# A hybrid decoder step on one core: where the accumulating transfers, the next block's tokens and a few copies are placed

## The chip, the cores and the metric

The kernel runs on one core of a Trainium2 chip. The metric is the time of one execution on the device in microseconds (us). Three runs of the kernel before took 2428.46, 2424.86 and 2425.33 us; the median is 2425.33.

## The reference

One inference step of a single decoder layer for 2048 prompt tokens and 64 sample tokens, width 1024, all in float32. An input projection feeds two mixers, a gated linear recurrence with matrix states (HGRN2) and a short gated convolution; an output projection, a layer norm, a feed-forward block and a second layer norm follow:

```python
mix = jnp.einsum('btm,md->btd', jnp.concatenate([o.astype(x.dtype), yc], axis=-1), w_out)
x = _layer_norm(ALPHA * x + mix, ln1_g, ln1_b)
hid = jnp.square(jax.nn.relu(jnp.einsum('btd,df->btf', x, w_ff1)))      # FF1, 1024 -> 4096
x = _layer_norm(ALPHA * x + jnp.einsum('btf,fd->btd', hid, w_ff2), ln2_g, ln2_b)   # FF2
```

## The kernel before

**Blocks and stages.** The prompt is worked off in four blocks of 512 tokens; block 1 also carries the 64 sample tokens. A block has two phases, each with a memory pool of its own. The "m" phase holds the input projections (`m1`, `m2`, `m3`), the recurrence that runs between their steps (`rec_step`), the output projection and the first layer norm. The "f" phase holds the feed-forward block. The hidden width is cut into eight chunks c of 512; chunks 0 and 1 are computed plainly at the start of the f phase (`pl["f0"]`), and then two parts follow, each with the rest of its four chunks: FF1 for them and then FF2 for all four. In time: block 0 has FF1 from about 290 us, FF2 from 333.9 to 428.1, FF1 to 515.2, FF2 to 597.0; the FF2 stages of block 1 are 993.3 to 1097.7 and 1188.5 to 1289.8, those of block 2 1613.7 to 1691.7 and 1772.3 to 1852.8.

**Precision by splitting.** Each float32 operand is split into a high part, copied by ScalarE (ACT) into the matmul's float32r type, and a low part, the rest, by VectorE (DVE): `wh`, `wl` for weights (lines 201 and 208), `h`, `l` for FF2's left operands, `X` for tokens, `hp` for sample operands (lines 162 and 163, in `split`). A product is three matmuls (high x high, high x low, low x high: lines 237 to 239, and 243 to 245 where several chains share a bank); the sample's pairs take two (248, 249). DVE's low parts are put into a list `later` and issued at the next `flush`, that is at the beginning of the next unit.

**Products by a fast scheme.** FF2 in every block, and FF1 in blocks 1 to 3, use a 2 x 2 scheme with seven products instead of eight, in this order:

```python
PRODUCTS = (("T4", "D"), ("B11", "A"), ("B21", "C"), ("T2", "A"), ("T1", "B"), ("T3", "A"), ("B22", "B"))
```

FF2 makes seven passes, one for each product, each over four chunks: 28 units of one weight tile each. After a pass's last chunk its two banks are added into the result tokens `x1` (`add_to`, lines 1229 and 1232), in T3 into two places each; four of the passes (`SAMPLE`) also have sample matmuls in block 1, and at their end `sample_sums` copies the upper half of a bank with ACT (`upper`, line 254, into a `TMP` tile) and adds both halves (lines 1240 to 1244). `sum_rows` forms FF2's left-hand sums (line 1221). `prepare` splits the left operand of a unit two units ahead into `h` and `l`, each in three buffers; in the f phase `TMP` takes its buffers from h's three.

**Sums of weights, made by transfers.** T1 to T4 are sums of weight quarters. They are made once, in HBM, by transfers from GpSimd's queue (POOL), some of which accumulate: `make_sums` yields after each. It makes T1 and T3 as copies, accumulates onto both, copies T3 to T2, accumulates, copies T2 to T4, accumulates. Every accumulation needs the transfer to the same tile before it: eight chunks, or six, earlier. `making` makes the 64 for FF2 (tiles T_b) during block 0's m phase; `making1` makes 48 for FF1 (six chunks, tiles T_a), which blocks 1 to 3 read. Before, `making1` is advanced three steps after each of the 8 units of block 0's first FF1 and two after each of the 16 of the second. Nothing in POOL's queue waits for those units, only for transfers.

**The weights' queue.** Weight and token tiles are "units" in one fixed list. SyncE's queue (SP) loads them into three `st` buffers, `unit_split` makes the parts, and `weights(i)` sees to it that units up to i + 3 are split. The next block's tokens are units too (`x_units`, four of them, a fifth for the sample ahead of block 1); `X_PLACES` says behind which FF2 units of the second part they stand. They take the `X` buffers that held this block's normed tokens. `norm_weights(1)` loads the second norm's `lnb` on SP's queue before the first FF2; that load has to wait for the last `affine` (line 943) of the first norm, and later weight loads stand behind it.

Of the kernel before, what the change touches and what calls it, by code (L numbers as in the profile page):

```python
# [9 lines left out]
F32 = mybir.dt.float32  # L10
# [3 lines left out]
ALU = mybir.AluOpType  # L14
AX = mybir.AxisListType

P = 128
# [28 lines left out]

SAMPLE = {"B21": (1, ((0, 1),)), "B11": (0, ((0, 1), (1, -1))), "T1": (0, ((1, 1),)), "B22": (1, ((1, 1),))}

X_PLACES = (("T3", 4), ("T3", 6), ("B22", 4), ("B22", 5), ("B22", 6))

QUARTER = {"B11": (0, 0), "B21": (1, 0), "B12": (0, 1), "B22": (1, 1)}

# [8 lines left out]
def hybrid_step(ctx, tc, a, o):  # L61
    nc = tc.nc
    v, s, g, te = nc.vector, nc.scalar, nc.gpsimd, nc.tensor

    cst = ctx.enter_context(tc.tile_pool(name="cst", bufs=1))
# [6 lines left out]
    def new(shape, tag, bufs, dt=F32, of=None):  # L72
        count[0] += 1
        return (of or pool).tile(list(shape), dt, tag=tag, bufs=bufs, name=f"{tag}{count[0]}")


    phase = {}
# [8 lines left out]
    def S(shape=(P, SLOT), dt=F32):  # L86
        assert phase["in"] == "m"
        return new(shape, "S", NSLOT, dt, phase["of"])

    def TMP():  # L90

        return S((P, 4, P)) if phase["in"] == "m" else new((P, 4, P), "h", 3, F32, phase["of"])

    def TOK(dt=F32):
        return new((P, D), "tok", 8, dt)
# [5 lines left out]
    def SM(shape):  # L101
        return new(shape, "sm", 16)
# [13 lines left out]
    small = cst.tile([P, 36], F32, name="small")  # L116
    lnb = cst.tile([P, 2, D], F32, name="lnb")
    nhalf = cst.tile([P, NH], F32, name="nhalf")
    halo = cst.tile([P, 4, 2], F32, name="halo")
    lw = cst.tile([P, 6, NH], F32, name="lw")  # L120
    lbl, onorm, convw = small[:, 0:4], small[:, 4:8], small[:, 8:20]
# [47 lines left out]
    def add_unit(src, scale=None, cols=D, use=None, spare=False):  # L169
        units.append((src, scale, cols, use, spare))  # L170
        return len(units) - 1
# [52 lines left out]
    def weights(i, kept=0):  # L224

        ahead(i + 4 - kept)
        return handles.pop(i)
# [4 lines left out]
    def pump():  # L232
        if bg:
            bg.pop(0)()
# [23 lines left out]
    def norm_weights(which):  # L258

        for i in range(2):  # L260
            nc.sync.dma_start(lnb[:, i, :], a["lnb"][:, 2 * which + i, :])
# [75 lines left out]
    def quarter2(c, k):  # L337
        return a["w_ff2"][c * 4 + RAW[k]] if k in RAW else sums[c][k]

    def make_sums(at, cs):  # L340
        for to, of, acc in (("T1", "B11", False), ("T3", "B22", False), ("T1", "B12", True), ("T3", "B12", True),
                            ("T2", "T3", False), ("T2", "B11", True), ("T4", "T2", False), ("T4", "B21", True)):
            for c in cs:
                if acc:
                    g.dma_start(at(c, to), at(c, of), accum_op=ALU.add, max_dma_last_dim=4096)
                else:
                    g.dma_start(at(c, to), at(c, of), max_dma_last_dim=4096)
                yield

    making = make_sums(quarter2, range(NCH))  # L350
    making1 = make_sums(quarter1, range(NPLAIN, NCH))

    for b in range(NB):
# [16 lines left out]
        for part in range(NCH // NPART):  # L370
# [9 lines left out]
            for step, _ in PRODUCTS:  # L380
                for c in cs:
                    ff2.append((step, c, add_unit(quarter2(c, step))))
                    if (step, c) in X_PLACES and nx:
                        src, cols, use = nx.pop(0)
# [13 lines left out]
    for b in range(NB):  # L398
# [20 lines left out]
        qs, ks, fs, scs, kds = {}, {}, {}, {}, {}  # L419
# [421 lines left out]
        def rec_step():  # L841
            nonlocal rec_done
            if not rec_done:
                rec_done = next(rec, 0) == 0

        def main():
            yield from m1()
            yield from m2()
            yield from m3()

        for i, _ in enumerate(main()):
            rec_step()
            if b == 0 and i >= 6:
                if i == 6:

                    g.tensor_tensor(SM((P, 1)), ks[0][:, 0:1], fs[0][:, 0:1], ALU.add)
                next(making, 0)
                next(making, 0)
            if i >= 16 and i % (3 if samp else 4) == 0:
                rec_step()  # L860
            if i % 2 == 0:
                pump()
# [71 lines left out]
        def drain():  # L934
            while lnq:
                before()
                after()
                flush()
# [71 lines left out]
        def F(shape, tag, bufs, dt=F32):  # L1010
            return new(shape, tag, bufs, dt, phase["of"])
# [10 lines left out]
        def values(c):  # L1022
            if c not in raw:

                raw[c] = F((P, 4, 2, 256), "raw", NPART)
            return raw[c]
# [170 lines left out]
        def prepare():  # L1197
            if not queue:
                return
            step, c = queue.pop(0)  # L1200
            r = raw[c]
            x = r[:, SLOT_OF[step]]
            h, l = F((P, 2, 256), "h", 3, F32R), F((P, 2, 256), "l", 3, F32R)
            split(h, l, x)
            hid[step, c] = (h, l)
            if step in SUMMED:
                assert (step, c) in summed
            seen.add((step, c))
            if step == PRODUCTS[-1][0]:
                del raw[c]  # L1210
# [35 lines left out]
        for part, (ff1_units, ff2_units) in enumerate(pl["parts"]):  # L1246
            queue += [(step, c) for step, c, _ in ff2_units]
            for i, (step, c, u) in enumerate(ff1_units):
                if i >= len(ff1_units) - 2:
                    prepare()  # L1250
                if b == 0:
                    if i == 0:
                        for _ in making:
                            pass
                    ff1(step, weights(u), segs)
                    for _ in range(3 - part):
                        next(making1, 0)
                else:
                    ff1_product(step, c, weights(u))
            drain()  # L1260
            if part == 0:
                norm_weights(1)
            else:
                xq.clear()
            sumq += [(k, c) for k in SUMMED for c in sorted({c for _, c, _ in ff2_units})]
            nsum = 0
            spairs = []
            squeue = [c * FC + 2 * SAMPLE[step][0] for step, c, _ in ff2_units if samp and step in SAMPLE]

            def sample_rows():  # L1270
                if squeue:
                    f = squeue.pop(0)
                    hp = F((P, 2, P), "hp", 2, F32R)
                    split(hp[:, :, 0:NS], hp[:, :, NS:P], sample_values(f // FC, f))
                    spairs.append(hp)

            banks = {}
            sample_rows()
            cfirst, clast = ff2_units[0][1], ff2_units[-1][1]
            for n_, (step, c, u) in enumerate(ff2_units):  # L1280
                w = weights(u)
                while sumq and (nsum * 3 + 6) // 2 <= n_:
                    sum_rows()
                    nsum += 1
                parts = [tuple(x[:, q * 512:q * 512 + 512] for x in w) for q in range(2)]
                prepare()
                if step in SAMPLE:
                    sample_rows()
                if pl["last"] and step == PRODUCTS[-1][0] and c >= NCH - 3:
                    if c == NCH - 3:  # L1290
                        last = [F((P, 4, 2, 256), "raw", NPART, F32R) for _ in range(2)]
                    for x in ((0, 2), (1, 3))[c - NCH + 3]:
                        split(last[0][:, x], last[1][:, x], raw[NCH - 1][:, x])
                k = to[step]
                first = k not in banks
                if first:
                    banks[k] = [PS() for _ in range(2)]
                h, l = hid.pop((step, c))
                for p in range(2):
                    cs = slice(p * P, p * P + P)  # L1300
                    for q, (rh, rl) in enumerate(parts):
                        mm3_on(banks[k][p], h[:, q, cs], l[:, q, cs], rh, rl, first and q == 0, c == clast and q == 1)
                if samp and step in SAMPLE:
                    if c == cfirst:
                        ys = PS()
                    hp = spairs.pop(0)
                    for q, (rh, rl) in enumerate(parts):
                        mm_pair(ys, hp[:, q, :], rh, rl, c == cfirst and q == 0, c == clast and q == 1)
                if c == clast:
                    for t0, dh, sign in INTO[k][step]:  # L1310
                        for p in range(2):
                            add_to(t0 + p, dh, banks[k][p], sign)
                    if samp and step in SAMPLE:
                        sample_sums(ys, SAMPLE[step][1])
# [4 lines left out]
        if b == NB - 1:  # L1319

            c = NCH - 1
            ws = [weights(u) for u in pl["last"]]
            flush_all()
            h, l = last
# [128 lines left out]
```

## Time and profile before

| What | us |
|---|---|
| median of three runs | 2425.33 |
| the profiled execution | 2427.2 |
| its span, first to last instruction | 2425.4 |
| TensorE (PE) busy | 2369.6 |
| VectorE (DVE) busy | 1729.7 |
| ScalarE (ACT) busy | 1212.1 |
| GpSimd (POOL) busy | 170.4 |

The times in the profile's rows come from the one profiled execution and count from its first instruction. A row of the timeline has start, duration, engine, line, operation, what it writes and reads, and in brackets how long the engine sat idle before it and what ended that. A row of waits has engine and line, whom it waited for, the sum in us, the number and the longest. A row of stretches has, after the stretch's bounds and length, the busy time of each engine, the granted share of TensorE's clock, the mean busy share of the core's 16 DMA engines, and GB/s. Rows of DMA queues give packets, MB and the share of the 16 engines' time (q1 is SP's queue with the weights, q0 POOL's); rows of issues give count, size and median us to landing.

### The profile page before, as it was taken

How to read it: one execution, taken by the hardware profiler on the slowest of the kernel's cores; microseconds unless marked ns; L12 is line 12 of the kernel's file. 1: busy time of each engine (PE TensorE's matmuls, PEld its weight loads, DVE VectorE, ACT ScalarE, POOL GpSimd, SP SyncE). 2: the span in 40 equal slices, each digit the busy share in tenths (PEclk: the TensorE clock that was granted, in tenths of full speed). 3: DMA queues.
4: the chain of work that ended last, by engine and by line, in shares of the span. 5: the costliest groups of instructions: out<-in, count | busy, mean ns of one | idle time of the engine just before them, and what ended most of it. 6: DMA issues, size and time to landing. Idle time of an engine off the chain costs nothing. (4 is left out here: it accounts for less than half of the span.)

```text
span 2425.4 us, 34901 instructions
## 1 busy us (share of the span) xinstructions
PE 2369.6 (98%) x13596; PEld 2062.5 (85%) x13596; DVE 1729.7 (71%) x2651; ACT 1212.1 (50%) x1898; POOL 170.4 (7%) x208
## 2 busy tenths in 40 slices
PE   8999989999999999899999999999999999999998
PEld 7888977887989889779977888998987888998996
DVE  7756648258775677775687856888588965888678
ACT  5234535355423446556654324665665324575563
POOL 2220321000001110000000000000000001000001
PEclk9999999999999999999999999999999999999999
DMA  8996999346223644444544325465566225456563
GB/s 294 273 273 213 286 280 284 115 136 200 100 65 84 164 153 131 158 154 160 172 147 140 100 70 182 152 205 186 179 191 191 99 76 170 141 196 193 182 189 116
DMA packets 128229, 412.40 MB, mean 170 GB/s; under 512 B 13184, under 2 KB 17664, under 8 KB 128064
## 3 DMA queue, kind: packets, MB, share of 16 engines
q1 hardware_dynamic: 105904, 342.19, 43.3%
q0 software_dynamic: 22016, 67.71, 11.1%
q8 instruction: 107, 1.75, 0.3%
q14 instruction: 58, 0.48, 0.1%
q10 hardware_dynamic: 144, 0.26, 0.0%
HBM read 399.07 MB, written 69.77 MB: 193 GB/s over the span
## 5 line engine op out<-in xcount | busy, mean ns | idle before, releaser
L208 DVE TENSOR_TENSOR wl<-st,wh 128x1024 fp32r<-128x1024 f32 x568 | 692.5, 1220 | 218.7 <-ACT wh L201 217.5
L201 ACT ACTIVATE wh<-st 128x1024 fp32r<-128x1024 f32 x569 | 600.4, 1055 | 401.5 <-PE ps L245 118.7
L237 PE MATMUL ps<-X,wh 128*128 128x256 f32 (+2 forms) x1504 | 515.2, 343 | 8.5 <-ACT X L162 8.0
L239 PE MATMUL ps<-X,wl 128*128 128x256 f32 (+2 forms) x1504 | 505.7, 336 | 0.3 <-DVE wl L208 0.3
L238 PE MATMUL ps<-X,wh 128*128 128x256 f32 (+2 forms) x1504 | 505.7, 336 | 0.3 <-DVE X L163 0.3
L245 PE MATMUL ps<-wh,l 128*128 128x512 f32 x868 | 345.3, 398 | 10.7 <-DVE l L163 10.4
L243 PE MATMUL ps<-wh,h 128*128 128x512 f32 x868 | 341.3, 393 | 10.3 <-ACT h L162 10.3
L244 PE MATMUL ps<-wl,h 128*128 128x512 f32 x868 | 341.2, 393 | 5.5 <-DVE wl L208 5.4
L237 PEld LDWEIGHTS ps<-X,wh 128*128 128x128 f32 x1504 | 286.2, 190 | 37.7 <-ACT X L162 8.9
L239 PEld LDWEIGHTS ps<-X,wl 128*128 128x128 f32 x1504 | 285.8, 190 | 27.5 <-DVE wl L208 0.7
L238 PEld LDWEIGHTS ps<-X,wh 128*128 128x128 f32 x1504 | 286.2, 190 | 26.2 <-DVE X L163 1.4
L245 PEld LDWEIGHTS ps<-wh,l 128*128 128x128 f32 x868 | 164.3, 189 | 60.5 <-DVE l L163 26.9
L243 PEld LDWEIGHTS ps<-wh,h 128*128 128x128 f32 x868 | 164.7, 190 | 44.3 <-ACT h L162 11.8
L244 PEld LDWEIGHTS ps<-wl,h 128*128 128x128 f32 x868 | 164.3, 189 | 42.3 <-DVE wl L208 7.8
L163 DVE TENSOR_TENSOR l<-raw,h 128x512 fp32r<-128x512 f32 x217 | 148.2, 683 | 19.7 <-ACT h L162 19.7
L269 POOL TENSOR_TENSOR sm<-sm,nhalf 128x1 f32<-128x1 f32 (+1 forms) x34 | 35.1, 1033 | 1579.5 <-DVE sm L268 1533.3
L162 ACT ACTIVATE h<-raw 128x512 fp32r<-128x512 f32 x217 | 133.6, 616 | 4.4 <-DVE tok L1244 2.3
L245 PE MATMUL ps<-X,wl 128*128 128x256 f32 (+1 forms) x432 | 124.9, 289 | 0.0
L243 PE MATMUL ps<-X,wh 128*128 128x256 f32 (+1 forms) x432 | 124.9, 289 | 0.0
L244 PE MATMUL ps<-X,wh 128*128 128x256 f32 (+1 forms) x432 | 124.9, 289 | 0.0
L1134 DVE TENSOR_TENSOR raw<-raw,ps 128x256 f32<-128x256 f32 (+1 forms) x96 | 50.4, 551 | 85.1 <-PE ps L245 84.9
L237 PE MATMUL ps<-wh,X 128*128 128x512 f32 x256 | 104.1, 407 | 0.0
(256 smaller groups left out, 4122.1 us busy)
## 6 DMA issues: line engine op xcount, KB each, us to landing
st<-in_w_ff SPq DMA_DIRECT2D x231, 512.0 KB, 3.6
st<-T_b SPq DMA_DIRECT2D x124, 512.0 KB, 3.9
st<-in_w_in SPq DMA_DIRECT2D x110, 512.0 KB, 3.5
st<-T_a SPq DMA_DIRECT2D x72, 512.0 KB, 3.6
st<-in_w_out SPq DMA_DIRECT2D x56, 512.0 KB, 4.5
T_b<-in_w_ff POOLq DMA_DIRECT2D x48, 512.0 KB, 18.4
T_a<-in_w_ff POOLq DMA_DIRECT2D x36, 512.0 KB, 23.7
T_b<-T_b POOLq DMA_DIRECT2D x16, 512.0 KB, 19.1
```

Of the source, the lines that this page charges most:

```text
L162: s.activation(hi, src, AF.Copy)
L163: later.append(lambda: v.tensor_tensor(lo, src, hi.bitcast(F32), ALU.subtract))
L201: s.activation(wh, st, AF.Copy)
L208: v.tensor_tensor(wl, st, wh.bitcast(F32), ALU.subtract)
L237: te.matmul(out, lh, rh, start=first, stop=False)
L238: te.matmul(out, lh, rl, start=False, stop=False)
L239: te.matmul(out, ll, rh, start=False, stop=last)
L243: te.matmul(out, lh, rh, start=first, stop=False, skip_group_check=True)
L244: te.matmul(out, lh, rl, start=False, stop=False, skip_group_check=True)
L245: te.matmul(out, ll, rh, start=False, stop=last, skip_group_check=True)
L269: g.tensor_tensor(st[:n, 15:16], st[:n, 14:15], nhalf[:n, 0:1], ALU.pow)
L1134: v.tensor_tensor(z, z, ps, (ALU.add, ALU.subtract)[op - 2])
```

## The change

Five edits. `hold` is a POOL addition of one column, x + x into a tile `tick`, that reads x and so waits for whoever writes x; POOL's later instructions stand behind it. In block 0's FF1, after each unit, one `hold` on the chunk's result and one step of `making1` (before: three or two steps without a read). In block 0's FF2, at each pass's first unit, a `hold` on that unit's h and one step. In block 1's projections one step at every second step of the loop. In all these are 24, 14 and up to 24 calls; the 48 transfers are used up in block 1. `TMP` in the f phase gets two buffers of its own. `X_PLACES` moves the tokens to one unit in a pass: behind chunk 6 of T4, B11, B21 and T3, and the fifth behind chunk 5 of B22 (before: two in T3 and the rest in B22). The first two `prepare` calls for FF2 come three FF1 units earlier. The `hold` helper also takes the place of one existing addition in block 0.

```diff
-X_PLACES = (("T3", 4), ("T3", 6), ("B22", 4), ("B22", 5), ("B22", 6))
+X_PLACES = (("T4", 6), ("B11", 6), ("B21", 6), ("T3", 6), ("B22", 5))
...
-        return S((P, 4, P)) if phase["in"] == "m" else new((P, 4, P), "h", 3, F32, phase["of"])
+        return S((P, 4, P)) if phase["in"] == "m" else new((P, 4, P), "tmp", 2, F32, phase["of"])
...
+    tick = cst.tile([P, 1], F32, name="tick")
...
+    def hold(x):
+
+        g.tensor_tensor(tick, x, x, ALU.add)
...
-                    g.tensor_tensor(SM((P, 1)), ks[0][:, 0:1], fs[0][:, 0:1], ALU.add)
+                    hold(ks[0][:, 0:1])
                 next(making, 0)
                 next(making, 0)
+            if b == 1 and i % 2 == 0:
+                next(making1, 0)
...
-                if i >= len(ff1_units) - 2:
+                if len(ff1_units) - 5 <= i < len(ff1_units) - 3:
                     prepare()
...
                     ff1(step, weights(u), segs)
-                    for _ in range(3 - part):
-                        next(making1, 0)
+                    hold(values(c)[:, 0, 0, 0:1])
+                    next(making1, 0)
...
                 h, l = hid.pop((step, c))
+                if b == 0 and n_ % 4 == 0:
+                    hold(h[:, 0, 0:1].bitcast(F32))
+                    next(making1, 0)
```

## The prediction

> **What bounds the kernel now.** I read the page first, then a table of stretches cut at the kernel's stages, then the waits and the timeline inside the stretches that were too long.
>
> ```profile
> span 2425.4 us, 34901 instructions
> PE 2369.6 (98%) x13596; PEld 2062.5 (85%) x13596; DVE 1729.7 (71%) x2651; ACT 1212.1 (50%) x1898; POOL 170.4 (7%) x208
> ```
>
> TensorE (PE) sets the end: it is busy 2369.6 of 2425.4 us, and the change leaves its matmuls as they are. So it can gain only what PE idles, about 56 us, plus slow matmuls after an idle. In the next rows the columns are stretch, PE, PEld, DVE, ACT, POOL busy, granted clock, DMA share, GB/s. The first row is most of block 0's way through FF1's start, the fourth its second FF1; all others are the second feed-forward product (FF2), 28 units of weights each: block 0 twice, block 1 twice, block 2 twice.
>
> ```profile
> 251.00:333.90 82.90, 82.90 (x524) 75.44 (x523) 45.69 (x56) 42.49 (x69) 24.75 (x32) 1.00 1.03 294
> 333.90:428.10 94.20, 82.32 (x337) 63.45 (x336) 64.93 (x81) 44.33 (x56) 14.87 (x18) 0.96 0.96 284
> 428.10:515.20 87.10, 87.10 (x386) 72.15 (x385) 25.13 (x24) 34.79 (x48) 0.00 (x0) 1.00 0.32 102
> 515.20:597.00 81.80, 79.66 (x338) 63.63 (x337) 68.13 (x86) 48.77 (x62) 0.00 (x0) 0.98 0.62 195
> 993.30:1097.70 104.40, 95.10 (x402) 76.86 (x402) 77.36 (x113) 50.84 (x79) 0.00 (x0) 0.97 0.49 161
> 1188.50:1289.80 101.30, 92.97 (x403) 74.68 (x401) 80.65 (x115) 54.95 (x82) 0.00 (x0) 1.00 0.52 166
> 1613.70:1691.70 78.00, 77.46 (x338) 62.63 (x337) 66.74 (x84) 45.87 (x58) 0.00 (x0) 1.00 0.61 196
> 1772.30:1852.80 80.50, 78.38 (x338) 62.61 (x337) 69.64 (x86) 48.19 (x60) 0.00 (x0) 1.00 0.65 201
> ```
>
> Block 2's first FF2, 78.0 us, has nothing of what is changed: it is the floor, 2.8 us a unit and 11.1 us a pass of four. Against it block 0 loses 16.2 and 3.8 us, block 2's second FF2 2.5 us. Block 1's two carry sample matmuls as well (402 and 403 against 338) and lose more.
>
> **Part 1: the accumulating transfers.** Why block 0's first FF2 is long:
>
> ```profile
> 346.46 0.80 PE L243 MATMUL ps<-wh,h 128*128 128x512 f32 x1 [6.92 <-ACT h L162]
> ...
> ACT wh L201 <- DMA st<-T_b: 26.5, 12, 9.4
> ...
> q1 hardware_dynamic: 4461, 16.24, 48.7%
> q0 software_dynamic: 4394, 10.40, 47.2%
> ...
> T_a<-in_w_ff POOLq DMA_DIRECT2D x12, 512.0 KB, 20.7
> T_a<-T_a POOLq DMA_DIRECT2D x6, 512.0 KB, 19.5
> ```
>
> PE waited 6.92 us for an h behind a weight copy on ACT, and ACT waited 26.5 us for weights to land: the 18 POOL transfers issued here took 47.2% of the DMA engines, beside 48.7% for weights. That is 0.472 x 94.2 / 18 = 2.5 us of all engines each. All 48 are issued in one burst, from 251 us on.
>
> After the change each waits behind a read of a result: 8 in the first FF1, 7 in the first FF2 (one a pass), 16 in the second FF1, 7 in the second FF2, 38 in all; the last 10 go, one every second step, into block 1's projections. In FF1 a unit takes 87.1 / 16 = 5.4 us, so one transfer a unit is cheap there; even the burst cost PE nothing in 251 to 333.9, at DMA share 1.03. In FF2 the share becomes about 0.61 + 2.5 / 11.1 = 0.84, where it was 0.96. Price of a transfer inside FF2: above, 16.2 / 18 = 0.9 us, so 6.3 us a stage; below, nothing, by the 251 row. I take 3.2 us in the first, between the ends but nearer to zero since transfers no longer queue behind each other, and since the two loads of lnb still stand ahead of the weights at its start; and 0.5 us in the second. First FF2: 78.0 + 3.2 = 81.2, **13.0 us less**.
>
> The reads add 38 GpSimd instructions. Nearest rows:
>
> ```profile
> L269 POOL TENSOR_TENSOR sm<-sm,nhalf x34: 540/900/1504, 221.5 to 2416.1; 128x1 f32<-128x1 f32 x32, 64x1 f32<-64x1 f32 x2
> ...
> L208 DVE TENSOR_TENSOR wl<-st,wh x568: 1205/1219/1253, 16.1 to 2392.7; 128x1024 fp32r<-128x1024 f32 x190
> ```
>
> One column on POOL takes 0.54 to 1.50 us, at most 38 x 1.5 = 57 us on an engine busy 170.4 us of the span: hidden. A read in FF2 keeps its h buffer (three in all) until POOL has come to it; h is made two units, 5.6 us, ahead of its use, so POOL must be that late before PE feels it. Behind a waiting read stand the next transfer and read. An accumulation waits for the transfer six earlier, 32 us in FF1 and 66 us in FF2 against 20.7 us to land. DVE's own update of an FF1 result waits for the read too, as do reuses of that buffer: at most 1.5 us against 5.4 us a unit. Cost taken: zero; bounds 0 and 14 x 0.96 us (below). In block 1 the 10 transfers pass ahead of the layer norm's small powers and output stores on POOL's queue, each an issue's length; PE has no stall there that I could charge, so zero.
>
> The Trainium skill, GPSIMD Engine Reference, Key points, says that GpSimd shares its SBUF interfaces with VectorE and contends with VectorE instructions that have two SBUF inputs; wl and l are such. If that cost DVE as much as POOL, the total would be about 2416 instead of 2402 (the rival below). The trace shows the contention on one side alone: POOL's read-like instruction spreads from 540 to 1504 ns while wl stays within 1205 to 1253.
>
> **Part 2: own buffers for the half copies.** Only block 1's FF2 makes such copies there (8, at the ends of sample passes) beside two in its transposes. The stall they stand beside:
>
> ```profile
> 1030.97 0.77 PE L248 MATMUL ps<-wh,hp 128*128 128x512 f32 x1 [3.34 <-DVE hp L163]
> ...
> 1024.94 0.60 ACT L254 ACTIVATE h<-ps 64x512 f32<-64x512 f32 x1 [2.07 <-PE ps L249]
> ...
> 1025.57 0.68 DVE L1243 SCALAR_TENSOR_TENSOR tok<-tok,ps 64x512 f32<-64x512 f32 x1 [0.85 <-ACT h L254]
> 1026.28 0.68 DVE L1244 TENSOR_TENSOR tok<-tok,h 64x512 f32<-64x512 f32 x1
> 1026.89 0.67 DVE L1243 SCALAR_TENSOR_TENSOR tok<-tok,ps 64x512 f32<-64x512 f32 x1
> 1027.60 0.68 DVE L1244 TENSOR_TENSOR tok<-tok,h 64x512 f32<-64x512 f32 x1
> 1028.21 1.21 DVE L208 TENSOR_TENSOR wl<-st,wh 128x1024 fp32r<-128x1024 f32 x1
> 1029.34 0.68 DVE L1221 SCALAR_TENSOR_TENSOR raw<-raw 128x512 f32<-128x512 f32 x1
> 1029.94 0.67 DVE L163 TENSOR_TENSOR l<-raw,h 128x512 fp32r<-128x512 f32 x1
> 1030.55 0.28 DVE L163 TENSOR_TENSOR hp<-tok,hp 128x128 fp32r<-128x128 f32 x1
> ```
>
> The copy on ACT (L254) waited for its matmul, not for a buffer, and from L1243 on DVE runs eight instructions without a gap to the hp that PE wants. Order on DVE makes this stall; another buffer takes no instruction out. Gain: between 0 and, were every such stall gone, about 13 us (3.34 us twice, four of about 1 us, slow matmuls behind them). I take **0**.
>
> **Part 3: the next block's tokens.** Where they stand now, block 2's second FF2 shows:
>
> ```profile
> 1843.92 0.50 PE L244 MATMUL ps<-wl,h 128*128 128x512 f32 x1 [1.98 <-DVE wl L208]
> ...
> 1793.24 0.69 DVE L1229 TENSOR_TENSOR tok<-tok,ps 128x512 f32<-128x512 f32 x1 [0.34 <-PE ps L245]
> 1794.60 0.69 DVE L1229 TENSOR_TENSOR tok<-tok,ps 128x512 f32<-128x512 f32 x1 [0.67 <-PE ps L245]
> ...
> 1840.26 2.47 DVE L1229 TENSOR_TENSOR tok<-tok,ps 128x512 f32<-128x512 f32 x4
> 1842.65 1.22 DVE L208 TENSOR_TENSOR wl<-st,wh 128x1024 fp32r<-128x1024 f32 x1
> ```
>
> Two token units in one pass make DVE reach that pass's four sums late (no idle ahead of them), and the wl behind them stalls PE 1.98 us. Spread, each pass gets one subtraction, like wl 1.22 us, and in the tight B11 pass DVE idles 0.34 + 0.67 = 1.01 us at its sums: 0.2 us too little, once or twice. Their SP transfers, as large as a weight's, move with them: five loads a pass instead of four, share 0.61 x 5/4 = 0.76. X buffers are free by then: FF1's matmuls that read them are over. Block 2: 80.5 to 78.4, **2.1 us less**. Block 0: 81.8 to 78.0 + 0.8 + 0.5 for POOL = 79.3, **2.5 less**. Block 1 had also:
>
> ```profile
> 1275.93 0.50 PE L244 MATMUL ps<-wl,h 128*128 128x512 f32 x1 [1.00 <-DVE wl L208]
> ...
> 1288.76 0.50 PE L248 MATMUL ps<-wh,hp 128*128 128x512 f32 x1 [2.19 <-DVE hp L163]
> ```
>
> 3.2 us and, by the 0.50 us matmuls behind them, some 1.6 us of slow clock: 101.3 to 96.5, **4.8 less**. Bounds of the three together: 3 and 12 us.
>
> **Part 4: two h's made three units earlier.** At the start of block 1's first FF2:
>
> ```profile
> 992.40 0.67 DVE L163 TENSOR_TENSOR l<-raw,h 128x512 fp32r<-128x512 f32 x1
> 993.00 1.39 DVE L943 TENSOR_TENSOR tok<-tok,lnb 64x512 f32<-64x512 f32 x2
> ...
> 1002.28 0.50 PE L243 MATMUL ps<-wh,h 128*128 128x512 f32 x1 [3.39 <-ACT h L162]
> ```
>
> No instruction more; the l leaves its place ahead of the layer norm's affine, so lnb's load, which waits for that, and the weights behind it come one l, 0.67 us, sooner. **0.6 less** there, zero elsewhere (what late weights hold up stays late).
>
> **Sum.** 13.0 + 2.5 + 4.8 + 2.1 + 0.6 = 23.0 us. The profiled execution took 2427.2 us (span 2425.4), so 2404.2; the median of the runs, 2425.33, is 1.9 below it: 2402.3, say **2402**.
>
> **Rivals.**
> - The half copies do hold ACT back and part 2 frees it: 13 us more, 2389. For it, h and copy share three buffers; against it, the gapless DVE rows. 0.10.
> - POOL's transfers hurt FF2 as before, 0.9 us each: 84.3 us in both of block 0's, so 3.1 + 5.0 us are lost from the sum: 2410. For it, share 0.84 is no light load. 0.13.
> - The spreading does nothing, since the weights behind lnb are late by themselves: 15.5 us fall out, 2418. Against it, 26.5 us of ACT's waits over 12 units, not at the start alone. 0.06.
> - Reads slow DVE by what POOL stretches, 1.504 - 0.540 = 0.96 us, 14 times in block 0's FF2: 13.4 us, 2416. 0.04.
> - Slower: POOL falls behind (transfers landing later than 66 us), and each read in FF2 holds its h past its use. From 5.6 us of lag on, ACT cannot make the next h; two units lost at 14 reads are 14 x 5.6 = 78 us, 2480; it decides from 1.6 us a read on. Against it: 20.7 us under worse load. 0.05.
>
> **How the numbers follow.** My forecast, 0.62, has a range of its own of 2393 to 2411 (FF2 with POOL's transfers 0 to 6.3 us, tokens 3 to 12). To keep 0.8 I take 2388 to 2416, which takes in the first two rivals. A measurement here can tell about 0.2%, 4.9 us: faster 0.92, same 0.03, slower 0.05.
>
> **What would show it.** Right: block 0's first FF2 near 81 us with ACT's waits for st a few us; POOL instructions up to 600 us and some beyond; the 3.34 us waits for hp still there; no wl wait ahead of the last pass. Wrong: an hp wait gone (part 2), h or raw waiting for POOL (slower), 84 us or more in both of block 0's FF2.

## The result and the profile after

The changed kernel takes 2411.34 us, the median of 4 runs (2409.64 to 2412.75), beside 2426.89 us for the kernel before in 4 runs. The ratio is 0.9935 with a 95% interval of 0.9917 to 0.9952: faster by 15.5 us. The profiled execution took 2410.24 us, with a span of 2408.4 us, 17.0 us less than the span before. Helpers stand one line further down in this kernel (the split is L163 and L164, the weights' parts L202 and L209), the matmuls of a bank with several chains are L244 to L246, the sample's L249; `sum_rows` is L1228, the sums at a pass's end are L1236 and L1239, the accumulating transfers L346, the copying ones L348, and the new read is L353.

First the page's span and engines of the kernel after, as the page of before was read:

```profile
span 2408.4 us, 34950 instructions
PE 2362.9 (98%) x13596; PEld 2059.6 (86%) x13596; DVE 1728.9 (72%) x2651; ACT 1209.1 (50%) x1898; POOL 189.3 (8%) x246
```

The matmuls are the same 13596; their busy time fell by 6.7 us and PE's idle time by 10.3 us. The same stretches as in the prediction, of the kernel after (stretch, length, PE, PEld, DVE, ACT, POOL busy, granted clock, DMA share, GB/s): block 0's first FF2, its second FF1, its second FF2, block 1's two FF2, block 2's two.

```profile
333.70:413.30 79.60, 78.17 (x338) 62.46 (x337) 63.75 (x80) 43.68 (x56) 9.34 (x12) 1.00 0.76 232
413.30:500.30 87.00, 87.00 (x385) 72.08 (x384) 25.13 (x24) 34.79 (x48) 19.74 (x34) 1.00 0.78 203
500.30:584.50 84.20, 79.27 (x338) 62.29 (x336) 69.01 (x86) 48.30 (x63) 9.76 (x13) 1.00 0.81 240
979.60:1084.60 105.00, 95.47 (x403) 77.05 (x402) 76.63 (x112) 50.37 (x79) 0.00 (x0) 0.97 0.50 160
1175.40:1274.60 99.20, 93.87 (x403) 75.87 (x402) 80.68 (x115) 54.43 (x83) 0.00 (x0) 0.98 0.55 175
1597.10:1675.20 78.10, 77.56 (x339) 62.63 (x338) 66.55 (x83) 45.98 (x58) 0.00 (x0) 1.00 0.61 196
1755.80:1835.60 79.80, 77.62 (x338) 62.61 (x337) 71.20 (x87) 50.23 (x62) 0.00 (x0) 1.00 0.69 214
```

Beside the forecast, in us:

| Stretch | before | forecast | after |
|---|---|---|---|
| block 0, first FF2 | 94.2 | 81.2 | 79.6 |
| block 0, second FF2 | 81.8 | 79.3 | 84.2 |
| block 1, first FF2 | 104.4 | 103.8 | 105.0 |
| block 1, second FF2 | 101.3 | 96.5 | 99.2 |
| block 2, second FF2 | 80.5 | 78.4 | 79.8 |
| span | 2425.4 | 2402.4 | 2408.4 |

So nearly all of the gain is one stretch, 14.6 us, and the second FF2 of block 0 became longer, not shorter. The five stretches add up to 14.4 us less; the other 2.6 us of the span's 17.0 came mostly in block 1's projections, 1.4 us ahead of its first FF2 and 1.4 us behind its second. What block 0's second FF2 waits for is seen in the timeline of PE of the kernel after (start, duration, then in brackets the idle time ahead and what ended it):

```profile
527.27 0.50 PE L246 MATMUL ps<-wh,l 128*128 128x512 f32 x1 [1.27 <-DVE l L164]
...
533.92 0.50 PE L246 MATMUL ps<-wh,l 128*128 128x512 f32 x1 [0.71 <-DVE l L164]
...
540.33 0.50 PE L246 MATMUL ps<-wh,l 128*128 128x512 f32 x1 [0.68 <-DVE l L164]
...
545.22 0.50 PE L246 MATMUL ps<-wh,l 128*128 128x512 f32 x1 [1.21 <-DVE l L164]
...
576.62 0.50 PE L246 MATMUL ps<-wh,l 128*128 128x512 f32 x1 [0.68 <-DVE l L164]
```

Five waits of PE for a low part l of DVE's. The last, behind the sums of T3, stands with the same 0.68 us in the kernels without these transfers (below), so four come with the transfers: two of them (527.27 and 540.33) soon after a pass's sums and two in the middle of a pass. ACT's waits in the same stretch say what made DVE late (engine, line, what it waited for, total, times, longest), and the rows of its transfers show the load. A row of DVE's timeline, ahead of the wait at 533.92, shows it idle for ACT's copy of such a weight:

```profile
ACT wh L202 <- DMA st<-in_w_ff: 13.0, 7, 3.0
ACT wh L202 <- DMA st<-T_b: 12.7, 5, 3.9
...
531.43 1.22 DVE L209 TENSOR_TENSOR wl<-st,wh 128x1024 fp32r<-128x1024 f32 x1 [2.48 <-ACT wh L202]
```

```profile
q1 hardware_dynamic: 4551, 16.32, 58.2%
q0 software_dynamic: 1626, 3.85, 22.3%
...
st<-T_b SPq DMA_DIRECT2D x12, 512.0 KB, 5.3
```

Weights came late: 25.7 us of ACT's waits, beside POOL's queue at 22.3% of the DMA engines. The four waits fall where that queue issues accumulations (L346) and not copies (L348). POOL's timeline in the kernel after, with the start of the first FF2's accumulations ahead, and then all that PE waited for l in the first FF2:

```profile
376.94 1.09 POOL L346 DMA_DIRECT2D T_a<-in_w_ff  x1
...
547.63 1.04 POOL L346 DMA_DIRECT2D T_a<-in_w_ff  x1
559.95 0.55 POOL L348 DMA_DIRECT2D T_a<-T_a  x1
...
PE ps L246 <- DVE l L164: 1.4, 3, 0.6
```

But the first FF2 has three accumulations too, from 376.94 us on, and its three waits for l come to 1.4 us only. There POOL's queue had 17.4%, ACT waited nearly as long for weights (12.5 and 10.3 us), and yet PE was busy 78.17 of 79.60 us.

### The profile page after: what moved, and what is told of

It is laid out like the page before. It is cut to its first block, busy times and chain, and to the rows that moved or that the text cites. A ratio compares the mean times of both kernels' runs of the same rounds, so it can differ in the third digit from the quotient of the medians.

```text
span 2408.4 us, 34950 instructions
## 1 busy us (share of the span) xinstructions
PE 2362.9 (98%) x13596; PEld 2059.6 (86%) x13596; DVE 1728.9 (72%) x2651; ACT 1209.1 (50%) x1898; POOL 189.3 (8%) x246
## 4 chain that ended last, share of the span: by engine, by line
PE 54%; DVE 2%; issue 1%; ACT 0%; DMA 0%; DVEq 0%; ACTq 0%
PE ps L246 10%; PE ps L245 10%; PE ps L244 10%; PE ps L238 7%; PE ps L240 7%; PE ps L239 7%; PE ps L682 1%; PE ps L249 1%; PE ps L250 1%; DMA st<-in_w_ff 0%; DVE wl L209 0%; DVE tok L1236 0%; DVE l L164 0%; PE ps L771 0%; PE ps L768 0%
## 5 line engine op out<-in xcount | busy, mean ns | idle before, releaser
L209 DVE TENSOR_TENSOR wl<-st,wh 128x1024 fp32r<-128x1024 f32 x568 | 692.6, 1221 | 197.4 <-ACT wh L202 195.7
L202 ACT ACTIVATE wh<-st 128x1024 fp32r<-128x1024 f32 x569 | 600.0, 1055 | 373.7 <-PE ps L246 106.9
L246 PE MATMUL ps<-wh,l 128*128 128x512 f32 x868 | 343.9, 396 | 14.4 <-DVE l L164 14.3
L244 PE MATMUL ps<-wh,h 128*128 128x512 f32 x868 | 340.2, 392 | 4.0 <-ACT h L163 4.0
L239 PEld LDWEIGHTS ps<-X,wh 128*128 128x128 f32 x1504 | 285.4, 190 | 25.7 <-DVE X L164 0.9
L246 PEld LDWEIGHTS ps<-wh,l 128*128 128x128 f32 x868 | 163.8, 189 | 63.4 <-DVE l L164 30.2
L244 PEld LDWEIGHTS ps<-wh,h 128*128 128x128 f32 x868 | 164.1, 189 | 37.8 <-ACT h L163 5.0
L164 DVE TENSOR_TENSOR l<-raw,h 128x512 fp32r<-128x512 f32 x217 | 148.5, 684 | 15.7 <-ACT h L163 15.7
L163 ACT ACTIVATE h<-raw 128x512 fp32r<-128x512 f32 x217 | 133.6, 616 | 2.5 <-PE ps L245 2.5
L246 PE MATMUL ps<-X,wl 128*128 128x256 f32 (+1 forms) x432 | 124.8, 289 | 0.0
L244 PE MATMUL ps<-X,wh 128*128 128x256 f32 (+1 forms) x432 | 124.7, 289 | 0.0
```

The costliest lines, as they stand in the source:

```text
L163: s.activation(hi, src, AF.Copy)
L164: later.append(lambda: v.tensor_tensor(lo, src, hi.bitcast(F32), ALU.subtract))
L202: s.activation(wh, st, AF.Copy)
L209: v.tensor_tensor(wl, st, wh.bitcast(F32), ALU.subtract)
L239: te.matmul(out, lh, rl, start=False, stop=False)
L244: te.matmul(out, lh, rh, start=first, stop=False, skip_group_check=True)
```

## Experiments

The kernels below are variations of the changed one; each diff is against it unless said otherwise. All but the last two are single executions: the span and the stretches of one profile, against the span of 2408.4 us; the four runs of the kernel after lie within 3.1 us. Block 0's second FF2 shows how far such a stretch repeats: in the kernel after and three others that leave it as it is, it was 84.2, 84.4, 86.6 and 86.7 us. Over the kernel after and the variations below, block 1's first FF2 takes 103.8 to 105.0 us wherever lnb's load and the order on DVE are as in the kernel after, and its second 97.2 to 99.9 us wherever that order and the token places are.

### The tokens back

```diff
-X_PLACES = (("T4", 6), ("B11", 6), ("B21", 6), ("T3", 6), ("B22", 5))
+X_PLACES = (("T3", 4), ("T3", 6), ("B22", 4), ("B22", 5), ("B22", 6))
```

> The changed kernel with the tokens at their old places (the rest of the change kept). In the changed kernel block 0's second FF2 takes 84.2 us, block 1's 99.2, block 2's 79.8. Theory A (transfers and early tokens load the DMA engines and VectorE in the same passes, T4 to B21, of block 0's second FF2): that stage falls to about 82 to 83 us, with its stalls moved from the passes T4 to B21 to the last two; block 2's goes back to 80.5 and block 1's to 101.3; span about 2410. Theory B (the transfers alone make block 0's stage long, wherever the tokens are): it stays at 84 or rises towards 88, as the old token stall of 2 us is added to it.

Span 2414.4 us. Two of its stretches, block 0's and block 2's second FF2:

```profile
502.00:586.50 84.50, 80.78 (x338) 63.60 (x337) 68.41 (x85) 47.26 (x61) 9.26 (x13) 0.98 0.79 231
...
1760.50:1841.30 80.80, 78.39 (x338) 62.50 (x337) 69.37 (x85) 47.94 (x60) 0.00 (x0) 1.00 0.63 200
```

Block 1's second FF2 went back to 102.7 us and block 2's to 80.8, so the spread tokens are worth 3.5 us (2.8 to 5.5 over the values above) and 1.0 us there. In block 0 they are worth nothing as long as the transfers run beside them: 84.5 against 84.2 to 86.7. With the old places the seven transfers cost 84.5 - 81.8 = 2.7 us.

### Block 0's second FF2 without transfers, and with its reads alone

```diff
-                if b == 0 and n_ % 4 == 0:
+                if b == 0 and part == 0 and n_ % 4 == 0:
```

> The changed kernel without reads and transfers in block 0's second FF2 (those seven transfers go later, into block 1's projections). Theory A: the stage falls from 84.2 to about 80, what block 2's second FF2 takes with the same token places (79.8); span about 2404. Rival C (the burst of transfers issued just ahead of the stage, at 486 to 490 us, or the token places alone make it long): it stays above 83 us.

and, keeping the reads,

```diff
                     hold(h[:, 0, 0:1].bitcast(F32))
-                    next(making1, 0)
+                    if part == 0:
+                        next(making1, 0)
```

> The changed kernel with the seven reads of h kept in block 0's second FF2 but their transfers moved to block 1. If the transfers' load makes the stage long, it falls to about 78.5 us, as without both; if the reads do (by holding h, or by slowing VectorE), it stays above 83 us.

Spans 2402.8 and 2400.1 us. Block 0's second FF2 with neither, and with the reads alone (two kernels, one stretch each):

```profile
502.00:580.50 78.50, 77.79 (x338) 62.62 (x337) 69.04 (x86) 49.48 (x63) 0.00 (x0) 1.00 0.66 211
```

```profile
500.20:578.40 78.20, 77.52 (x337) 62.52 (x336) 69.25 (x87) 48.61 (x62) 9.35 (x7) 1.00 0.67 211
```

The reads cost nothing. The transfers cost 84.2 - 78.35 = 5.9 us, 0.84 us each, and the stretch without them is the forecast's 78.0 + 0.8 less half a microsecond. With the reads alone the weights from T_b land 3.6 us after issue instead of 5.3, and ACT's waits for st are 17.2 us instead of 25.7. PE's one wait for l that is left in each, 0.68 us, is the one behind the sums of T3. The two spans differ by 2.7 us, 1.2 us of it ahead of block 0's first FF2 (which starts at 335.8 and 334.6 us), where the two kernels are the same; nothing is read from that.

### Three transfers, mostly in passes without a token unit

```diff
-                if b == 0 and n_ % 4 == 0:
+                if b == 0 and n_ % 4 == 0 and (part == 0 or n_ in (12, 16, 24)):
```

> The changed kernel, in block 0's second FF2 with reads and transfers only at the first units of T2, T1 and B22, the passes that have no whole token unit of the next block's prompt or no sums; the other four transfers go to block 1. If transfers cost only where a token unit stands in the same pass, the stage takes 78.2 to 79.3 us (78.5 us without any); if each costs 0.8 us wherever it is, 80.5 to 81.5 us.

Its stretch, and a row of POOL's timeline:

```profile
500.40:582.10 81.70, 79.28 (x338) 62.35 (x337) 68.62 (x86) 48.23 (x62) 6.10 (x7) 1.00 0.73 221
...
565.58 2.08 POOL L346 DMA_DIRECT2D T_a<-in_w_ff  x2
```

Three transfers stand in the passes T2, T1 and B22, of which only B22 has a token; the first of block 1's goes out right behind the last of them (565.58 us, x2). These four cost 81.7 - 78.35 = 3.4 us, 0.85 us each, as much as each of the seven; all four are accumulations. So a token unit listed in the same pass isn't what makes a transfer dear (its load may still fall into the next pass).

### The burst back, with and without the earlier h's

```diff
-            if b == 1 and i % 2 == 0:
-                next(making1, 0)
...
-                    hold(values(c)[:, 0, 0, 0:1])
-                    next(making1, 0)
+                    for _ in range(3 - part):
+                        next(making1, 0)
...
-                if b == 0 and n_ % 4 == 0:
-                    hold(h[:, 0, 0:1].bitcast(F32))
-                    next(making1, 0)
```

> The changed kernel with the transfers issued in one burst again, as before the change: three and two after each FF1 unit, no reads in FF1 and FF2, nothing in block 1. My theory: block 0's first FF2 goes back to 93 to 95 us, its second falls to 78 to 79 us, the rest stays; span about 2417. Rival (the earlier two h's, not the transfers, shortened the first FF2): it stays below 85 us.

and, besides that,

```diff
-                if len(ff1_units) - 5 <= i < len(ff1_units) - 3:
+                if i >= len(ff1_units) - 2:
```

> The changed kernel with the burst of transfers as before the change and the two h's made late as before (tokens and half copies stay changed). With the burst and early h's block 0's first FF2 took 90.5 us, where the kernel before had 94.2. If the early h's gave those 3.7 us, the stage goes back to 93.5 to 95 us with a wait of 5 to 7 us at its third unit. If it is only how the transfers fell that time, it stays between 89 and 92 us.

Spans 2413.2 and 2415.6 us. Block 0's first FF2 in the one kernel as a stretch, and its first wait for an h in PE's timeline; then both in the other:

```profile
334.00:424.50 90.50, 83.01 (x338) 62.78 (x338) 64.48 (x80) 44.32 (x56) 16.06 (x19) 0.98 0.98 295
```

```profile
341.10 0.50 PE L244 MATMUL ps<-wh,h 128*128 128x512 f32 x1 [1.45 <-ACT h L163]
```

```profile
333.30:427.30 94.00, 82.40 (x337) 63.57 (x336) 64.82 (x81) 44.43 (x56) 15.22 (x18) 0.95 0.95 288
```

```profile
345.68 0.79 PE L244 MATMUL ps<-wh,h 128*128 128x512 f32 x1 [6.75 <-ACT h L163]
```

With the burst and late h's the stretch is what it was before, 94.0 us (before: 94.2), with its long wait for h, 6.75 us. The earlier h's alone take that wait to 1.45 us and the stretch to 90.5; the spread transfers take it on to 79.6. So of the 14.6 us, 3.5 belong to part 4, 10.9 to part 1 and 0.2 to neither, taken in this order: what the earlier h's are worth once the transfers are spread, no run shows. The first of the two fits neither of its expectations, 93 us or more and below 85; both parts share the gain. The second FF2 with the burst was 78.5 and 78.1 us: all of its transfers were over by then.

### The half copies in h's buffers again

```diff
-        return S((P, 4, P)) if phase["in"] == "m" else new((P, 4, P), "tmp", 2, F32, phase["of"])
+        return S((P, 4, P)) if phase["in"] == "m" else new((P, 4, P), "h", 3, F32, phase["of"])
```

> The changed kernel with the half copies taking h's buffers again. My theory (the 3.3 us stalls in block 1 come from the order of VectorE's instructions): block 1's two FF2 stages stay within 0.5 us of 105.0 and 99.2, with both 3.3 us waits for hp; the span stays within 1 us of 2408.4. Rival (own buffers do free ScalarE): the stages grow by 1 us or more.

Block 1's two FF2 in this kernel took 104.9 and 99.7 us (after: 105.0 and 99.2), and the wait for hp stands in both, in the kernel after first, then in this one:

```profile
1017.67 0.77 PE L249 MATMUL ps<-wh,hp 128*128 128x512 f32 x1 [3.35 <-DVE hp L164]
```

```profile
1020.11 0.47 PE L249 MATMUL ps<-wh,hp 128*128 128x512 f32 x1 [3.35 <-DVE hp L164]
```

The span was 2410.9 us, 2.5 us longer and not within the 1 us that was expected; the excess is that of block 0's second FF2, 86.7 us, which has no sample and so none of its half copies. Part 2 changes nothing that can be measured.

### The low parts ahead of the sums

If DVE's order makes that wait, then issuing the pending low parts ahead of a pass's sums must take it away:

```diff
                 if c == clast:
+                    flush()
```

(in the FF2 loop, ahead of the `add_to` calls)

> The changed kernel with the pending low parts issued on VectorE ahead of the sums at each pass's end instead of behind them. My theory (order on VectorE makes the stalls after a pass): both 3.3 us waits for hp in block 1 and the waits of 0.5 to 1.3 us for l after passes go; block 1's FF2 stages fall by 4 to 7 us each, block 2's first FF2 from 78.1 to about 77.3; span 2390 to 2398. Rival (the sums only get late instead, and the banks that they free): stalls for banks or sums take their place, span 2405 or more.

Span 2387.4 us, 21.0 less. All of PE's waits for l and hp in the whole kernel after, and then in this one:

```profile
PE ps L246 <- DVE l L164: 14.3, 19, 1.3
...
PE ps L249 <- DVE hp L164: 6.7, 2, 3.3
```

```profile
PE ps L246 <- DVE l L164: 4.2, 6, 1.2
...
PE ps L249 <- DVE hp L164: 1.1, 1, 1.1
```

DVE's timeline at the same place in this kernel, and then the stretches of block 1's two FF2 and block 2's first; after them block 0's second FF2 and block 2's second:

```profile
1009.60 0.28 DVE L164 TENSOR_TENSOR hp<-tok,hp 128x128 fp32r<-128x128 f32 x1
1009.80 1.28 DVE L1239 SCALAR_TENSOR_TENSOR tok<-tok,ps 128x512 f32<-128x512 f32 x2
```

```profile
978.40:1075.10 96.70, 94.03 (x402) 76.77 (x402) 77.03 (x113) 50.36 (x78) 0.00 (x0) 0.96 0.53 175
1166.00:1258.60 92.60, 91.45 (x402) 74.81 (x402) 81.05 (x116) 54.35 (x82) 0.00 (x0) 1.00 0.59 188
1581.10:1657.40 76.30, 76.30 (x338) 62.91 (x337) 67.08 (x84) 45.95 (x58) 0.00 (x0) 1.00 0.64 205
...
497.60:581.70 84.10, 79.81 (x337) 63.59 (x336) 68.97 (x86) 47.89 (x63) 10.20 (x13) 0.98 0.78 237
1738.00:1817.60 79.60, 77.82 (x339) 62.61 (x339) 70.80 (x87) 50.36 (x62) 0.00 (x0) 1.00 0.66 213
```

The l and hp now stand ahead of the sums and both 3.3 us waits are gone; one of 1.1 us is left. Even the stretch that the prediction took as the floor, block 2's first FF2, went from 78.1 to 76.3 us, with PE busy throughout. But the last two stretches stay as they were, 84.1 against 84.2 and 79.6 against 79.8 us, and the 4.2 us of waits for l that are left all stand in these two. So there the order on DVE is not what sets the time.

### A read of its own for each FF1 unit

`hold` reads a column that only the first of each chunk's four units writes, and a group of four transfers goes at once. POOL's timeline in the kernel after:

```profile
318.99 0.19 POOL L353 TENSOR_TENSOR tick<-raw 128x1 f32<-128x1 f32 x1 [16.88 <-ACT raw L1054]
...
319.45 0.66 POOL L348 DMA_DIRECT2D T_a<-in_w_ff  x1 [0.27 <-issue]
...
322.71 1.16 POOL L348 DMA_DIRECT2D T_a<-in_w_ff  x1
```

```diff
-                    hold(values(c)[:, 0, 0, 0:1])
+                    hold(values(c)[:, step % FC // 2 * 2, step % 2, 0:1])
```

> The changed kernel with each FF1 read on a column that its own unit wrote last, so that one transfer goes out after each unit. In the changed kernel they go out in fours, once a chunk, and five together at 486 to 490 us, ahead of block 0's second FF2. If that burst makes the stage long, it falls from 84.2 to 82 us or less; if the transfers issued inside the stage do (my theory, from the run without them, 78.5 us), it stays between 83 and 87 us, and block 0's first FF2 near 79.6 us.

Span 2412.4 us; block 0's two FF2 took 79.5 and 86.6 us. The groups at the end of FF1 cost the first FF2 nothing, and they are not what makes the second long.

### The load of lnb later

```diff
-            if part == 0:
-                norm_weights(1)
...
+                if part == 0 and n_ == 12:
+                    norm_weights(1)
```

(the second place is in the FF2 loop, ahead of the unit's `weights`)

> The changed kernel with the second norm's lnb loaded after twelve units of the first FF2 instead of ahead of it. My theory (the weight load behind lnb's, which waits for the last affine, makes the 3.6 us wait at the start of block 1's first FF2): that wait and the 0.6 us behind it go, the stage falls from 105.0 to about 101 us, block 0's first FF2 by 0.5 us, span about 2404. Rival (weights are late there by themselves): it stays above 103.5 us.

Span 2404.3 us. PE's longest wait in block 1's first FF2 in the kernel after, and then all of its waits there in this one:

```profile
PE ps L244 <- ACT h L163: 3.6, 1, 3.6
...
```

```profile
PE ps L249 <- DVE hp L164: 3.3, 1, 3.3
PE ps L246 <- DVE l L164: 2.0, 2, 1.3
```

The wait for h at the start is gone and the stretch is 100.1 us instead of 105.0; block 0's first FF2 is 78.0 instead of 79.6, which is the floor, with all its transfers in it (78.5 to 79.6 us in the seven kernels with these transfers, the load of lnb ahead and the order on DVE as in the kernel after).

### The best version

Three of these edits together: no steps and reads in block 0's second FF2, the low parts ahead of the sums, lnb later.

> Four pieces together: the changed kernel without reads and transfers in block 0's second FF2, with lnb loaded after twelve units, and with the pending low parts issued ahead of the sums. From the single runs: low parts first gave a span of 2387.4 us; the second FF2 of block 0 should fall by 5.6 us and block 1's first by 3 to 5. I expect 2375 to 2381 us. If the pieces share the same gain, 2384 us or more.

It takes 2379.0 us, the median of 4 runs (2376.84 to 2380.81), beside 2426.79 for the kernel before; the ratio is 0.9804, 0.9791 to 0.9818. The three edits alone took 5.6, 21.0 and 4.1 us off the span, in all 30.7, and together 2408.4 - 2376.2 = 32.2: they add up. Its stretch of block 0's first FF2:

```profile
334.10:410.50 76.40, 76.40 (x338) 63.00 (x337) 64.20 (x81) 43.90 (x56) 8.81 (x12) 1.00 0.77 241
```

PE is busy throughout, and block 2's first FF2, without any transfers, takes 76.3 us in the same kernel. So in block 0's first FF2 the spread transfers cost nothing.

The same with the tokens moved once more, away from the tight passes B11 and B21:

```diff
-X_PLACES = (("T4", 6), ("B11", 6), ("B21", 6), ("T3", 6), ("B22", 5))
+X_PLACES = (("T4", 6), ("T1", 6), ("T3", 6), ("B22", 5), ("B22", 6))
```

> As the run with four pieces, with the tokens behind T4, T1, T3 and B22 instead of T4, B11, B21 and T3. VectorE forms FF2's sums from T4 to T1, and B22 has none, so if VectorE's load makes the token units cost, block 2's second FF2 falls from 79.6 to 77 to 78 us, and the time is 2 to 4 us below that of the run with four pieces; if only the loads on the DMA engines count, it is the same within 1 us.

2378.18 us in 5 runs (2377.83 to 2380.2), ratio 0.9802, 0.9789 to 0.9815: not to be told from the version above. Block 2's second FF2 took 78.8 us against 79.3, not 77 to 78. That fits what was expected if only the loads on the DMA engines count, and not DVE's work.

## Why the prediction was right, and where its steps were not

The sum had 23.0 us, the span gave 17.0, the medians 15.5. The direction, the place of the gain and its mechanism held; of the sum's five terms one was too small and four were too large. The median, 2411.34 us, lies inside the stated range of 2388 to 2416, but just outside the forecast's own, 2393 to 2411, which its named ends (0 to 6.3 us for the transfers, 3 to 12 for the tokens) would put at 2396 to 2418 if both stages are counted. It is close to what the second rival gave, 2410, by another road: one of the two stretches cost what that rival says, the other nothing, and the tokens gave too little. So part of the hit is luck. One sign also failed to come: ACT's waits for weights in the first FF2 were to be a few us and were 22.8. (In the prediction's first table the third row, not the fourth, is block 0's second FF1; no sum uses that.)

**Part 1, first FF2: right, by terms that were off.** 13.0 us were forecast and 14.6 came. The 3.2 us were taken for the transfers and the loads of lnb together. The transfers' part is zero, the lower bound, as the best version shows; lnb's loads are the rest, 0.5 to 1.6 us. And part 4's earlier h's, counted as zero in block 0 ("what late weights hold up stays late"), gave 3.5 us with the burst in place: with the h's made ahead, the late weights no longer hold up the matmuls that wait for an h behind them on ACT.

**Part 1, second FF2: the step that failed.** "I take 0.5 us in the second" is the mis-sized term: the seven transfers cost 5.9 us, 0.84 us each, near the upper bound of 0.9 (and up to 8.4 us in the kernels where the stretch took 86.7). So the rival by which transfers hurt FF2 as before was right in this stretch and wrong in the other. The reason given for the low value, that transfers no longer queue behind each other, is true (over the whole kernel the transfers from w_ff to T_a land in 7.8 us in the median, before in 23.7), but weights still came late. Nearly the same transfers cost nothing at DMA share 0.77 and 5.9 us at 0.81. What sets that apart stays open. Spread tokens and transfers together cost more than each alone (transfers at the old tokens' places 2.7 us, from one execution each; the new places without transfers a gain of 3.4, both together a loss of 2.4), yet transfers moved mostly out of the tokens' passes cost as much each; accumulations, beside which the waits stand, ran in the first FF2 as well; and the low parts ahead of the sums left the stretch at 84.1 us. What wasn't tried is a second FF2 of block 0 with transfers and without any tokens.

**The reads: right.** L353 took 0.19 to 1.18 us, nothing waited for it, and in the second FF2 the reads alone left 78.2 us. wl on DVE kept its median, as the row of the kernel after shows (shortest, median and longest ns):

```profile
L209 DVE TENSOR_TENSOR wl<-st,wh x568: 1204/1219/1258, 15.2 to 2375.7; 128x1024 fp32r<-128x1024 f32 x190
```

So the loss that the rule of the Trainium skill's GPSIMD Engine Reference (Key points) could have brought, 2416 us, did not come. The times of POOL's reads do spread, but no run shows that this is contention. The step that read the pacing as one transfer a unit was wrong, since four units share the column read; the kernel with a column for each unit was no faster.

**Part 2: right.** Zero was forecast; taking the buffers back changed nothing, and changing DVE's order removed the wait. What the prediction priced at up to 13 us, "were every such stall gone", gave 8.3 and 6.6 us in block 1 alone, and 21.0 us in all.

**Part 3: right in kind, too large.** Forecast 2.5, 4.8 and 2.1 us. In block 0 the tokens' own gain was 3.4 us without the transfers, and none beside them. In block 1 both waits that the prediction showed are gone, but the stretch lost only 2.1 us: PE's busy time in it rose by 0.9 us, from 92.97 to 93.87 (granted clock 1.00, then 0.98), and the longest wait for l grew from 0.70 to 1.29. The projections behind it lost 1.4 us (190.3 to 188.9), with the clock at their start. Their first 5.2 us before, then after:

```profile
1289.80:1295.00 5.20, 5.20 (x17) 4.14 (x16) 4.38 (x9) 1.54 (x2) 0.07 (x1) 0.67 0.42 128
```

```profile
1274.60:1279.80 5.20, 5.20 (x25) 4.30 (x24) 4.29 (x8) 1.54 (x2) 0.09 (x1) 1.00 0.14 26
```

So the slow clock that the prediction priced at 1.6 us stood behind the stretch and not in it. It went with the wait of 2.19 us at the stretch's end: with the tokens back that wait was 0.95 us, the clock 1.00 and the projections 188.9 us. In block 2 part 3 gave 0.7 us. There the wait ahead of the last pass is gone, as forecast, and two others stand behind the sums of T4 and B11 in its place. PE's timeline in the kernel after, then DVE's:

```profile
1771.07 0.50 PE L246 MATMUL ps<-wh,l 128*128 128x512 f32 x1 [0.96 <-DVE l L164]
...
1782.94 0.50 PE L246 MATMUL ps<-wh,l 128*128 128x512 f32 x1 [0.68 <-DVE l L164]
```

```profile
1767.05 1.28 DVE L1236 TENSOR_TENSOR tok<-tok,ps 128x512 f32<-128x512 f32 x2
```

The prediction saw that a tight pass is "0.2 us too little", and let that cost nothing. DVE does come to the sums with no idle time ahead of them, and the l stands behind: 0.96 + 0.68 us, close to the 1.98 us that went away. But the place behind the sums is not the cause: with the low parts ahead of them the stretch still took 79.6 us and PE's waits for l in it 1.7 us instead of 2.2, and tokens moved away from B11 and B21 gave 78.8. The cause of what is left stays open.

**Part 4 in block 1: wrong, small.** 0.6 us less were forecast, 0.6 more came, which is within the 1.2 us by which that stretch varies. The wait for h stayed (3.4 us before, 3.6 after), since lnb's load still stands ahead of the weights on SP's queue and still waits for DVE's affine; moving that load took the wait away.

## What to carry to other kernels

Price a background transfer in the stage where it runs, not once for all: much the same transfers cost 0 us in one stage and 5.9 us in its near copy, and leaving those seven out of it was worth that much. Where a low part that the matmuls want stands behind sums that nobody waits for, ask for the order on the engine before the buffers: one line that issued the pending parts first was worth 21.0 us, more than the whole change, though nothing in the two stretches with late loads. A load that has to wait for another engine holds up every load behind it on its queue, so it belongs where nothing urgent follows.

## What was not expected of the hardware

Two things. A POOL read of one column waits for the last writer of just that column, so its pacing came in groups of four, and a group of them beside FF1 cost PE nothing at DMA share 0.78 (87.00 of 87.00 us busy). And a transfer's cost to PE did not follow the mean DMA share: none at 0.77 in block 0's first FF2 of the best version, 3.4 us at 0.73 in the second FF2 with the four accumulations.
